# A scan phase whose matmul order is written out by a planner of two streams, with whole groups of small matmuls, instead of left to the scheduler

## The chip, the cores and the metric

One core of one Trainium2 chip runs the whole program in one launch. The metric is device time in microseconds (us), the median over runs. TensorE is called PE here, its weight loads PEld, VectorE DVE, ScalarE ACT, GpSimd POOL, and SyncE, which issues the DMAs, SP.

## The reference, cut to what matters

The program computes two layers of a hybrid block over 512 tokens, 256 latent and 256 context, of width 1024. Each layer is a gated feed-forward half step, a token mixer of three branches (grouped attention, a two-way RWKV-7 scan, neighbourhood attention) and a second feed-forward half step. The change is in the RWKV branch:

```python
def rwkv_scan(state0, xs, emit):
    def step(state, inp):
        r_t, w_t, k_t, v_t, a_t, b_t = inp
        sa = einsum('zbhvk,zbhk->zbhv', state, a_t)
        state = state * w_t + sa * b_t + v_t * k_t
        out = einsum('zbhvk,zbhk->zbhv', state, r_t)
        return state, out
    return lax.scan(step, state0, xs)

y_ctx = scan(zeros, context tokens);  y = scan(state after the context, latent tokens)
readout: (group_norm(o forward + o backward) + bonus) * g
```

It has 8 heads of 64 channels and two directions z, forward and backward. The gates of the merge are `sigmoid(u @ w_in[gate columns])`, one 1024-wide set for each branch.

## The kernel before, in words

Channels lie on the 128 partitions, tokens along the free axis. Each large product is made from values split in two: `wload` (L262, L263) or `split` (L278, L279) turns a weight tile into a high part (ACT copy, `whi` or `phi`) and a low part (DVE subtraction, `wlo` or `plo`), and `gemm` (L272 to L274) issues three matmuls for each 128 rows of weights, on 512 columns (256 in layer 1 where only the latent tokens are needed).

The RWKV branch (`rwkv`) is the **scan phase** of a layer. It begins with four projections (`ps_first`), and then works on four **pairs** of heads, `ct` = 0 to 3, each in these stages:

- `rwkv_prep`: three projections of the pair (`proj`: k, v, r), a token shift of each, the key's norm (`rstd`: `ps_ss`, a POOL power, `ps_bc`), values per chunk (`ps_v` into `X`), the bonus; then `rwkv_dir` for each direction z: the decay and rate products (`ps_w` L949, `ps_a` L953), activations and a running sum, then `bk`, the two keys in one tile. `gram` (`ps_g`, L1041, evacuated to `G` at L1045) makes the 64x64 blocks of 8 chunks; then DVE multiplies `bk` in place by the chunk's decay (L1003) and PE transposes it (`ps_kb`, L1011).
- `inverse`: triangular inverses of the 64x64 blocks. DVE cuts the 16x16 diagonal blocks out (L1076), a DMA through DRAM lays those of both directions into one tile `N`, 15 steps of two tiny DVE instructions (L1096, L1098) invert them all, a DMA through DRAM brings them back (`cc`). Then for z = 0 and after it for z = 1: DVE masks `G` to `lt` (L1120), and five groups of small matmuls with an evacuation between each two: `ps_x`, `ps_it`, `ps_iw` (64x64), `ps_x2`, `ps_w2` (32x32), all five in the one bank `ia`.
- `rwkv_chain`, `chain_steps`: eight serial steps over the chunks. A step is four small matmuls `ps_z` (L1182), an ACT copy `zs`, four `ps_u` (L1203), copies into `X` (ACT L1205, DVE L1206), four `ps_h` (L1210), a DVE add into the next `X` (L1218); outputs `ps_oo` (L1191, L1224) beside them. `hq` (L1197) is the state times the chunk's decay, four DVE instructions a step.
- `rwkv_out`: the group norm and the gate (`ps_gg`, L1241); the result `yf` stays in SBUF until the attention phase.

The small products are in plain fp32, and a row of the trace counts two records for one such matmul.

**Fillers.** 42 projections that the rest of the mixer needs (queries, keys, values of the attention branches, gates) are cut into 8 **quanta** each, 336 in a layer (`spare_quanta`): a quantum is three matmuls `ps_gate` (L773 to L775), and after the eighth the tile goes to DRAM (`pd`). `fill(n)` emits n of them; `FILL` says how many after each pair, `LEFT` (8 and 2 tiles) how many are kept for the attention phase.

**What sets the order.** The kernel is written in Tile, whose scheduler arranges each engine's instructions from the order of emission, the dependences and a priority; `prio(-30)` is around the chain. So PE's order, one matmul at a time, is the scheduler's:

```python
            if ct < 3:
                for _ in self.rwkv_prep(ct + 1, nxt):
                    pass
                self.inverse(nxt["z"])
            with self.prio(-30):
                for _ in chain:
                    pass
            self.rwkv_out(ct, st, po, y)
            self.fill(min(8 * FILL[l][1 + ct], len(self.fq) - 8 * LEFT[l]))
```

Of the kernel before, what the change touches and what calls it, by code (L numbers as in the profile page):

```python
# [7 lines left out]
F32 = mybir.dt.float32  # L8
# [35 lines left out]
FILL = [[5, 7, 3, 4, 24], [8, 5, 4, 4, 24]]  # L44
# [7 lines left out]
    0, 4, 5, 6, 10, 14, 18, 19, 20, 21, 25, 29, 33)  # L52


class Program:
# [261 lines left out]
    def rstd(self, sqs, n, cols, scale, eps, tag="aux"):  # L317
# [5 lines left out]
        for k, sq in enumerate(sqs):  # L323
            for b in range(n):
# [5 lines left out]
                                in1=self.mhalf[:, 0:n * w].rearrange("p (n w) -> p n w", n=n), op=ALU.pow)  # L330
        bc = self.bank(tag, [P, n * P], "ps_bc")
# [193 lines left out]
    def proj(self, tile_i, full):  # L525

        nc = self.nc
        pt = self.bank("mm", [P, NT], "ps_p")
        for h in range(2):
            raw = self.rp.tile([P, NT], F32, tag="praw", name="praw", bufs=2)  # L530
# [3 lines left out]
            w = [[t[:, P * k:P * k + P] for k in range(4)] for t in (wh, wl)]  # L534
            self.gemm(pt[:, full], w, [t[:, full] for t in self.uh[4 * h:4 * h + 4]],
                      [t[:, full] for t in self.ul[4 * h:4 * h + 4]], h == 0, h == 1)
        return pt
# [265 lines left out]
    def fill(self, n):  # L803

        for _ in range(min(n, len(self.fq))):
            self.fq.pop(0)()


    def shift(self, i, full, pt=None):

        nc, l = self.nc, self.l
        if pt is None:
            pt = self.proj(T_R + i, full)
# [13 lines left out]
    def t(self):  # L827
        return self.rp.tile([P, NT], F32, tag="t", name="t", bufs=4)

    def rwkv(self):  # L830
# [25 lines left out]
        for h in HALVES:  # L856
            for w, pt in zip(ws, pts):
# [5 lines left out]
        self.gdt = self.shift(T_GD - T_R, tok)  # L863
        nc.scalar.activation(out=self.gdt[:, tok], in_=self.gdt[:, tok], func=AF.Tanh, scale=0.5)
        nc.vector.tensor_scalar(out=self.gdt[:, tok], in0=self.gdt[:, tok], scalar1=0.5, scalar2=0.5,
                                op0=ALU.mult, op1=ALU.add)
        self.fq = self.spare_quanta()
        self.fill_to = self.rp, "gm"
        st = {}
        y = []  # L870
        for _ in self.rwkv_prep(0, st):
            pass
        self.inverse(st["z"])
        self.fill(8 * FILL[l][0])
        for ct in range(4):
            nxt = {}
            po, chain = self.rwkv_chain(ct, st)

            if ct < 3:
                for _ in self.rwkv_prep(ct + 1, nxt):  # L880
                    pass
                self.inverse(nxt["z"])
            with self.prio(-30):
                for _ in chain:
                    pass
            self.rwkv_out(ct, st, po, y)
            self.fill(min(8 * FILL[l][1 + ct], len(self.fq) - 8 * LEFT[l]))
            st = nxt
        self.fill(len(self.fq) - 8 * LEFT[l])
        return y  # L890

    def rwkv_prep(self, ct, st):
        nc, l, tok, need = self.nc, self.l, self.tok, self.need
        pr = self.rwp[:, l]
        lora = self.rp.tile([P, 2, P], F32, tag="lora", name="lora")
        nc.sync.dma_start(out=lora, in_=self.A["lora"][l, ct][:, 0:2, :])
        g2 = self.rp.tile([P, P], F32, tag="g2", name="g2")
        nc.sync.dma_start(out=g2, in_=self.A["lora"][l, ct][:, 2, :])
        pk, pv = self.kv0 if ct == 0 else (None, None)
        k = self.shift(T_RK - T_R + ct, FULL, pk)  # L900
        yield
        v = self.shift(T_RV - T_R + ct, FULL, pv)
        yield
        r = self.shift(ct, tok)
        yield
        sq = self.t()
        nc.scalar.activation(out=sq, in_=k, func=AF.Square, scale=pr[:, 4, ct:ct + 1])
        bc = self.rstd([sq], 4, self.hsel, 1.0, 1e-12)
        kk = self.rp.tile([P, NT], F32, tag="kk", name="kk", bufs=1)
        nc.vector.scalar_tensor_tensor(out=kk, in0=k, scalar=pr[:, 4, ct:ct + 1], in1=bc, op0=ALU.mult, op1=ALU.mult)  # L910
        st.update(g2=g2)
        yield
# [9 lines left out]
        for p in range(2):  # L922
            o = slice(HD * (1 - p), HD * (1 - p) + HD)
            nc.scalar.activation(out=X[o, 0:4, 0, p, :], in_=pv[o, 4:8, :], func=AF.Copy)
            nc.scalar.activation(out=X[o, 4:8, 0, p, :], in_=pv[o, 0:4, :], func=AF.Copy)
            nc.vector.tensor_copy(X[o, :, 1, p, :], pv[o, ::-1, :])
        st["X"] = X
# [7 lines left out]
        st["z"] = []  # L935
        for z in range(2):
            yield
            st["z"].append((yield from self.rwkv_dir(ct, z, r, k, kk, lora)))

    def rwkv_dir(self, ct, z, r, k, kk, lora):  # L940
        nc, l, tok, need = self.nc, self.l, self.tok, self.need
        pr = self.rwp[:, l]
        rows = slice(64 * z, 64 * z + 64)
# [4 lines left out]
        pw = self.bank("aux", [P, NT], "ps_w")  # L948
        nc.tensor.matmul(pw, lora[rows, 0, :], self.wdt[rows, :], start=True, stop=True)  # L949
        sw = self.t()  # L950
        nc.scalar.activation(out=sw, in_=pw, func=AF.Tanh, scale=0.5, bias=self.wah[:, l, z, ct:ct + 1])
        pa = self.bank("aux", [P, NT], "ps_a")
        nc.tensor.matmul(pa, lora[rows, 1, :], self.adt[rows, :], start=True, stop=True)  # L953
        ta = self.t()
        nc.scalar.activation(out=ta, in_=pa, func=AF.Tanh, scale=0.5, bias=self.wah[:, l, 2 + z, ct:ct + 1])
        nc.gpsimd.tensor_scalar(out=sw, in0=sw, scalar1=1.0, scalar2=None, op0=ALU.add)
        S = self.t()
# [13 lines left out]
        yield  # L971
        inv = self.t()
# [3 lines left out]
        pc = self.rp.tile([P, NCH], F32, tag="pc", name="pc", bufs=4)  # L976
        nc.vector.tensor_copy(pc, ch(Q)[:, :, last])
# [14 lines left out]
        bk = self.rp.tile([P, NCH, 2, C], F32, tag="bk", name="bk", bufs=1)  # L992
# [4 lines left out]
        yield  # L997
        G = self.gram(z, bk, ar)
        yield

        pcb = pc.unsqueeze(2).to_broadcast([P, NCH, C])
        for x in range(2):
            nc.vector.tensor_tensor(out=bk[:, :, x, :], in0=bk[:, :, x, :], in1=pcb, op=ALU.mult)  # L1003
        kb = []
        flat = bk.rearrange("p j x t -> p (j x t)")
        for p in range(2):
            h = slice(HD * p, HD * p + HD)
            pt = self.bank("aux", [P, NCH, C], "ps_kb")
            t = self.lp.tile([P, NCH, C], F32, tag="kb", name="kb", bufs=5)
# [13 lines left out]
        return dict(ar=ar, kb=kb, G=G, pc=pc)  # L1023

    def gram(self, z, bk, ar):


        nc = self.nc
        nr = NCH if self.need else NCH // 2
# [18 lines left out]
        return G  # L1048
# [7 lines left out]
    def it(self):  # L1056
        return self.rp.tile([P, NT], F32, tag="it", name="it", bufs=3)

    def inverse(self, dirs):


        nc, tc = self.nc, self.tc
        halves = [slice(0, HD), slice(HD, P)]

        def ch(a):
            return a.rearrange("p (j t) -> p j t", t=C)

        dn = tc.dram_tile([NCH, 2, P, 16], F32, name="dn")
        dr = tc.dram_tile([2, NCH, 2, P, 16], F32, name="dr")
        for z in range(2):  # L1070
            G = dirs[z]["G"]
            e = self.it()
            for p in range(2):
                h = halves[p]
                for jh in range(2):
                    nc.vector.tensor_tensor(  # L1076
                        out=ch(e)[h, 4 * jh:4 * jh + 4].rearrange("p j (b t) -> p j b t", b=4),
                        in0=G[p][jh][h, :, 0:C].rearrange("p j (b t) -> p j b t", b=4),
                        in1=self.mblk[h].unsqueeze(1).unsqueeze(3).to_broadcast([HD, 4, 4, 16]), op=ALU.mult)
            if z == 1:  # L1080
                e1 = self.it()
                nc.vector.transpose(e1, e)
                e = e1
            ec = self.rp.tile([P, NCH, 16], F32, tag="ec", name="ec", bufs=2)
            nc.vector.tensor_reduce(out=ec, in_=e.rearrange("p (j b t) -> p j t b", j=NCH, b=4), axis=AX.X, op=ALU.add)
            nc.sync.dma_start(out=dn[:, z].rearrange("j g t -> g j t"), in_=ec)
        N = self.rp.tile([P, 16, 16], F32, tag="N", name="N", bufs=1)
        nc.sync.dma_start(out=N, in_=dn.rearrange("j z (g s) t -> (j z g) (s t)", s=16))
# [13 lines left out]
        for z in range(2):  # L1102
            d = dirs[z]
            G = d["G"]
            full = []
            for tag, i, bufs in (("W", z, 4), ("T", 1 - z, 1)):
                c = self.rp.tile([P, NCH, 16], F32, tag="ec", name="cc", bufs=2)
                nc.sync.dma_start(out=c, in_=dr[i, :, z].rearrange("j g t -> g j t"))
                t = self.rp.tile([P, NCH, C], F32, tag=tag, name=tag, bufs=bufs) if tag == "W" else ch(self.it())
                nc.vector.tensor_tensor(  # L1110
                    out=t.rearrange("p j (b t) -> p j b t", b=4),
                    in0=c.unsqueeze(2).to_broadcast([P, NCH, 4, 16]),
                    in1=self.mblk.unsqueeze(1).unsqueeze(3).to_broadcast([P, NCH, 4, 16]), op=ALU.mult)
                full.append(t)
            W, T = full
            lt = ch(self.it())
            for p in range(2):
                h = halves[p]
                for jh in range(2):
# [20 lines left out]
            def rows(p, blk):  # L1140
                return slice(HD * p + blk.start, HD * p + blk.stop)
# [307 lines left out]
```

## Time and profile before

| | |
|---|---|
| median of 3 runs | 2935.11 us (2932.16 to 2943.57) |
| the profiled execution's own time | 2933.89 us |
| its span in the profile | 2932.1 us |
| mean granted clock of TensorE, full speed as 1 | 0.971 |
| PE, DVE, ACT, POOL busy, share of the span | 95%, 60%, 36%, 9% |
| layer 0, first `ps_first` to last `ps_gg` | 426.48 to 963.92 us |
| layer 1, first `ps_first` to last `ps_gg` | 2071.21 to 2538.92 us |

A row of the timeline merges neighbouring instructions of one group (xN); its start is measured, a matmul's end is modelled, so what a matmul costs PE is read from the distance between starts. A share of busy time is a mean over stages with different limits.

### The profile page before, as it was taken

How to read it: one execution, taken by the hardware profiler on the slowest of the kernel's cores; microseconds unless marked ns; L12 is line 12 of the kernel's file. 1: busy time of each engine (PE TensorE's matmuls, PEld its weight loads, DVE VectorE, ACT ScalarE, POOL GpSimd, SP SyncE). 2: the span in 40 equal slices, each digit the busy share in tenths (PEclk: the TensorE clock that was granted, in tenths of full speed). 3: DMA queues.
4: the chain of work that ended last, by engine and by line, in shares of the span. 5: the costliest groups of instructions: out<-in, count | busy, mean ns of one | idle time of the engine just before them, and what ended most of it. 6: DMA issues, size and time to landing. Idle time of an engine off the chain costs nothing. (4 is left out here: it accounts for less than half of the span.)

```text
span 2932.1 us, 48565 instructions
## 1 busy us (share of the span) xinstructions
PE 2795.4 (95%) x19654; PEld 2229.4 (76%) x19654; DVE 1766.0 (60%) x3023; ACT 1068.6 (36%) x1928; POOL 277.6 (9%) x274
## 2 busy tenths in 40 slices
PE   7999999999999899999999999999899999898998
PEld 5788887656666666697888888888876678777998
DVE  4667346756674256757673477633578777485654
ACT  3223235323232246433222333222543433374543
POOL 0000011100000111230000110001210110022000
PEclk8999999999999999999999999999999999799998
DMA  7555343221112433336553365433432224344654
GB/s 277 201 187 170 107 134 105 76 69 44 41 58 73 133 108 110 105 119 215 171 181 106 119 201 183 147 102 107 141 114 69 70 60 119 104 130 138 218 177 144
DMA packets 205311, 376.59 MB, mean 128 GB/s; under 512 B 79776, under 2 KB 109088, under 8 KB 205088
## 3 DMA queue, kind: packets, MB, share of 16 engines
q1 hardware_dynamic: 205088, 373.51, 41.1%
q8 instruction: 154, 2.52, 0.4%
q14 instruction: 69, 0.57, 0.1%
HBM read 340.93 MB, written 31.46 MB: 127 GB/s over the span
## 5 line engine op out<-in xcount | busy, mean ns | idle before, releaser
L262 ACT ACTIVATE whi<-raw 128x1024 fp32r<-128x1024 f32 (+1 forms) x399 | 415.1, 1041 | 1102.5 <-PE ps_o L273 297.5
L263 DVE TENSOR_TENSOR wlo<-raw,whi 128x1024 fp32r<-128x1024 f32 (+1 forms) x399 | 500.4, 1255 | 425.1 <-ACT whi L262 415.8
L195 DVE SCALAR_TENSOR_TENSOR acc<-araw,cs,acc 128x1024 f32<-128x1024 f32 x210 | 260.6, 1279 | 14.3 <-DMA araw<-in_w_ada 14.0
L272 PE MATMUL ps_o<-hh,whi 128*128 128x512 f32 (+1 forms) x770 | 268.8, 349 | 0.0
L274 PE MATMUL ps_o<-hh,wlo 128*128 128x512 f32 (+1 forms) x770 | 268.0, 348 | 0.0
L273 PE MATMUL ps_o<-hl,whi 128*128 128x512 f32 (+1 forms) x770 | 266.6, 346 | 0.0
L272 PE MATMUL ps_fg<-uh,whi 128*128 128x512 f32 (+1 forms) x704 | 255.4, 363 | 7.3 <-ACT whi L262 3.7
L773 PE MATMUL ps_gate<-uh,whi 128*128 128x512 f32 (+1 forms) x672 | 255.6, 380 | 3.1 <-ACT whi L262 3.1
L274 PE MATMUL ps_fu<-uh,wlo 128*128 128x512 f32 (+1 forms) x704 | 251.9, 358 | 5.1 <-DVE wlo L263 5.1
L774 PE MATMUL ps_gate<-ul,whi 128*128 128x512 f32 (+1 forms) x672 | 256.0, 381 | 0.0
L274 PE MATMUL ps_fg<-uh,wlo 128*128 128x512 f32 (+1 forms) x704 | 253.4, 360 | 1.7 <-DVE wlo L263 1.7
L775 PE MATMUL ps_gate<-uh,wlo 128*128 128x512 f32 (+1 forms) x672 | 254.4, 379 | 0.7 <-DVE wlo L263 0.6
L273 PE MATMUL ps_fg<-ul,whi 128*128 128x512 f32 (+1 forms) x704 | 252.7, 359 | 0.1
L272 PE MATMUL ps_fu<-uh,whi 128*128 128x512 f32 (+1 forms) x704 | 251.2, 357 | 0.9 <-ACT whi L262 0.9
L273 PE MATMUL ps_fu<-ul,whi 128*128 128x512 f32 (+1 forms) x704 | 250.9, 356 | 0.0
L272 PEld LDWEIGHTS ps_fg<-uh,whi 128*128 128x128 f32 x704 | 134.8, 191 | 38.3 <-ACT whi L262 12.0
L272 PEld LDWEIGHTS ps_o<-hh,whi 128*128 128x128 f32 x770 | 144.7, 188 | 20.4 <-ACT whi L262 1.7
L273 PEld LDWEIGHTS ps_o<-hl,whi 128*128 128x128 f32 x770 | 144.5, 188 | 20.1
L274 PEld LDWEIGHTS ps_o<-hh,wlo 128*128 128x128 f32 x770 | 144.7, 188 | 18.2
L274 PEld LDWEIGHTS ps_fu<-uh,wlo 128*128 128x128 f32 x704 | 133.7, 190 | 26.6 <-DVE wlo L263 8.0
L773 PEld LDWEIGHTS ps_gate<-uh,whi 128*128 128x128 f32 x672 | 130.2, 194 | 28.3 <-issue 5.7
L274 PEld LDWEIGHTS ps_fg<-uh,wlo 128*128 128x128 f32 x704 | 134.7, 191 | 22.2 <-DVE wlo L263 3.0
(298 smaller groups left out, 5270.2 us busy)
## 6 DMA issues: line engine op xcount, KB each, us to landing
raw<-in_ffn_wi SPq DMA_DIRECT2D x176, 512.0 KB, 3.6
araw<-in_w_ada SPq DMA_DIRECT2D x144, 512.0 KB, 3.8
raw<-in_w_in SPq DMA_DIRECT2D x92, 512.0 KB, 3.7
raw<-in_ffn_wo SPq DMA_DIRECT2D x70, 448.0 KB, 3.3
raw<-in_ffn_wo SPq DMA_DIRECT2D x35, 512.0 KB, 3.5
pd<-fg SPq DMA_DIRECT2D x52, 256.0 KB, 2.0
raw<-in_w_branch SPq DMA_DIRECT2D x24, 512.0 KB, 3.8
praw<-in_w_in SPq DMA_DIRECT2D x44, 256.0 KB, 2.8
```

The source lines that it names most:

```text
L195: nc.vector.scalar_tensor_tensor(out=a, in0=raw, scalar=c, in1=a, op0=ALU.mult, op1=ALU.add)
L262: nc.scalar.activation(out=hi[:, :m], in_=r, func=AF.Copy)
L263: self.lo = nc.vector.tensor_tensor(out=lo[:, :m], in0=r, in1=hi[:, :m].bitcast(F32), op=ALU.subtract)
L272: nc.tensor.matmul(pt, wh, xh[k], start=first and k == 0, stop=False)
L273: nc.tensor.matmul(pt, wh, xl[k], start=False, stop=False)
L274: nc.tensor.matmul(pt, wl, xh[k], start=False, stop=last and k == n - 1)
L773: nc.tensor.matmul(pt, wh, xh, start=k == 0, stop=False)
L774: nc.tensor.matmul(pt, wh, xl, start=False, stop=False)
L775: nc.tensor.matmul(pt, wl, xh, start=False, stop=k == KD - 1)
```

## The change

The scan phase's PE order becomes the program's own. `tc.manual_schedule` takes PE from the scheduler between `ps_first` and the end of the phase; the other engines stay with it. The stages are generators: each `yield cost, after` ends a **whole group** of PE work, with an estimate of its length and of the time until the next group's inputs are there. `Streams.step` keeps a clock of its own and takes the first stream that is ready within 0.3, the chain ahead of the preparation; with none ready it emits one quantum (counted as 1.0, in layer 1 0.75). What the order rests on are these estimates, not semaphores. Beside that:

- two streams: `chains()` runs the four chains, `preps()` the directions, gram, keys and inverses; for a pair, `blocks(ct)` (the 16x16 step and the inverses) runs beside `rest(ct)` (keys of z = 1, and the three projections, norm and values of pair ct + 1). `preps` waits for the half of the chain of ct - 1 before the gram of z = 1.
- both directions' `ps_w` and `ps_a` come in pairs of banks; the two inverses go group by group side by side, z = 0 in bank `ia`, z = 1 in `aux`.
- the mask moves from `G` (DVE, four instructions per direction) to the evacuation of `ps_x`, which moves from ACT to DVE with it.
- `bk` times the decay moves from DVE to POOL and stands behind the last gram matmul that reads `bk`.
- `hq` is two DVE instructions for a step instead of four.
- `FILL` is gone; quanta that no gap took are emitted behind the phase. `LEFT` is as before.
- `yf` goes to DRAM (`yd`) and comes back in the attention phase, 4 DMAs each way and layer; `proj` takes its raw weights in the shared `raw` tiles; buffers: `t` 5 (4), `it` 4 (3), `bk` 2 (1), `kb` 6 (5).

```diff
+class Streams:
+    NEAR = 0.3
...
+    def par(self, *gens):
+        ready = {g: self.t for g in gens}
+        while ready:
+            g = min(ready, key=ready.get)
...
+                cost, after = next(g)
...
+            end = self.t + cost
+            ready[g] = end + after
+            yield cost, max(0.0, min(ready.values()) - end)
+
+    def step(self, streams):
...
+        g = next((g for g in live if self.ready.get(g, 0.0) <= self.t + self.NEAR), None)
+        if g is None and self.fill(1):
+            self.t += self.cost
+            return True
+        if g is None:
+            g = min(live, key=lambda g: self.ready[g])
+        self.t = max(self.t, self.ready.get(g, 0.0))
...
+            cost, after = next(g)
...
+        self.t += cost
+        self.ready[g] = self.t + after
...
+        mix = Streams(lambda n: len(self.fq) > left and self.fill(n), 1.0 if need else 0.75)
...
+        def blocks(ct):
+            st = sts[ct]
+            yield from self.blocks16(st)
+            yield from mix.par(*[self.inverse(st, z, ("ia", "aux")[z]) for z in range(2)])
+            done["prep"] = ct
+
+        def rest(ct):
+            while done["chain"] < ct - 1:
+                yield 0.0, 0.5
+            yield from self.keys(sts[ct]["z"][1])
+            if ct < 3:
+                yield from heads(ct + 1)
...
+            for ct in range(4):
+                st = sts[ct]
+                yield from self.rwkv_dirs(ct, st)
+                yield from self.gram(st, 0)
+                yield from self.keys(st["z"][0])
+                while done["half"] < ct - 1:
+                    yield 0.0, 0.5
+                yield from self.gram(st, 1)
+                yield from mix.par(blocks(ct), rest(ct))
...
+        streams = [chains(), preps()]
+        with self.tc.manual_schedule(engines={mybir.EngineType.PE}):
+            while mix.step(streams):
+                pass
+        self.fill(len(self.fq) - left)
...
-        pcb = pc.unsqueeze(2).to_broadcast([P, NCH, C])
-        for x in range(2):
-            nc.vector.tensor_tensor(out=bk[:, :, x, :], in0=bk[:, :, x, :], in1=pcb, op=ALU.mult)
...
+            if jh == 0:
+                pcb = d["pj"].unsqueeze(2).to_broadcast([P, NCH, C])
+                for x in range(2):
+                    nc.gpsimd.tensor_tensor(out=bk[:, :, x, :], in0=bk[:, :, x, :], in1=pcb, op=ALU.mult)
+            yield 1.2, 1.4
...
+        yield 0.0, 23.0
...
-                    nc.vector.tensor_tensor(out=lt[h, 4 * jh:4 * jh + 4], in0=G[p][jh][h, :, 0:C],
-                                            in1=self.mlev[h, z, :].unsqueeze(1).to_broadcast([HD, 4, C]), op=ALU.mult)
...
-            px = mm("ps_x", lt, T)
-            nc.scalar.activation(out=X, in_=px, func=AF.Copy)
+        px = mm("ps_x", lambda p, h, j: G[p][j // 4][h, j % 4, 0:C], T)
+        nc.vector.tensor_tensor(out=X, in0=px, in1=self.mlev[:, z, :].unsqueeze(1).to_broadcast([P, NCH, C]),
+                                op=ALU.mult)
+        yield 1.15, 1.1
...
-                    for z, p in units:
-                        nc.vector.tensor_scalar(out=hq[halves[p], z, :], in0=X[halves[p], s, z, p, :],
...
+                    for h in halves:
+                        nc.vector.tensor_tensor(
+                            out=hq[h], in0=X[h, s, :, halves.index(h), :],
+                            in1=st["pc"][h, s, :].unsqueeze(2).to_broadcast([HD, 2, C]), op=ALU.mult)
+            yield (s, 0.45, 0.8) if first else (s, 0.9, 0.4)
...
+            yield s, 0.45, 0.9
...
+            yield (s, 0.9, 1.0) if out else (s, 0.45, 1.4)
...
+        nc.sync.dma_start(out=self.yd[ct][:, tok], in_=os_[:, tok])
...
+                    yf = self.mp.tile([P, NT], F32, tag="qk", name="yf", bufs=4)
+                    nc.sync.dma_start(out=yf[:, tok], in_=self.yd[ct][:, tok])
```

What the change moves on PE is seen at two places. **Chain.** PE in layer 0, the chain of pair 0, before: the seventh step, from its `ps_oo` (L1191) on; `ps_gate` are quanta.

```order
L1191 MATMUL ps_oo<-ar,X 64x64 x3
L774 MATMUL ps_gate<-ul,whi 128x512
L775 MATMUL ps_gate<-uh,wlo 128x512
L773 MATMUL ps_gate<-uh,whi 128x512
L1203 MATMUL ps_u<-zs,W 64x64
L774 MATMUL ps_gate<-ul,whi 128x512
L1203 MATMUL ps_u<-zs,W 64x64
L775 MATMUL ps_gate<-uh,wlo 128x512
L1203 MATMUL ps_u<-zs,W 64x64
L773 MATMUL ps_gate<-uh,whi 128x512
L1203 MATMUL ps_u<-zs,W 64x64
```

The same chain now, one step from its `ps_z` (L1325) to its `ps_h` (L1353):

```order
L1325 MATMUL ps_z<-X,G 64x64 x4
L1333 MATMUL ps_oo<-ar,X 64x64 x4
L834 MATMUL ps_gate<-uh,whi 128x512
L835 MATMUL ps_gate<-ul,whi 128x512
L836 MATMUL ps_gate<-uh,wlo 128x512
L1346 MATMUL ps_u<-zs,W 64x64 x4
L834 MATMUL ps_gate<-uh,whi 128x512
L835 MATMUL ps_gate<-ul,whi 128x512
L836 MATMUL ps_gate<-uh,wlo 128x512
L1353 MATMUL ps_h<-X,kb 64x64 x4
```

Before, four matmuls of `ps_u` stand one by one among quantum matmuls; now each of the chain's groups stands whole, with one quantum of three matmuls between two groups.

**Inverse.** PE in layer 0, the inverse of pair 0, z = 0, before (L1127 are its 64x64 groups, 16 matmuls each; `ps_bo`, `ps_w` belong to the preparation of pair 1):

```order
L1127 MATMUL ps_x<-it 64x64
L773 MATMUL ps_gate<-uh,whi 128x512
L774 MATMUL ps_gate<-ul,whi 128x512
L1127 MATMUL ps_x<-it 64x64 x15
L775 MATMUL ps_gate<-uh,wlo 128x512
L773 MATMUL ps_gate<-uh,whi 128x512
L774 MATMUL ps_gate<-ul,whi 128x512
L775 MATMUL ps_gate<-uh,wlo 128x512
L1127 MATMUL ps_it<-it,W 64x64 x16
```

The inverses of pair 0 now (L1267 the 64x64 groups of both directions, L1291 the 32x32 ones; `ps_p` is a projection, `ps_ss`, `ps_bc`, `ps_v` belong to the norm and values of pair 1):

```order
L321 MATMUL ps_p<-uh,plo 128x512
L1267 MATMUL ps_x<-it,G 64x64 x32
L1267 MATMUL ps_it<-it,W 64x64 x16
L381 MATMUL ps_ss<-c_hsel,t 128x2 x4
L1267 MATMUL ps_it<-it,W 64x64 x16
L1267 MATMUL ps_iw<-W,it 64x64 x32
L395 MATMUL ps_bc<-c_ident,rs 64x128 x8
L1291 MATMUL ps_x_4432<-it,G 32x32 x16
L1032 MATMUL ps_v<-c_center,sh 64x64 x16
L1291 MATMUL ps_x_4476<-it,G 32x32 x16
```

Before, one direction's groups come with quanta between them and a single matmul ahead of the other fifteen; now the groups of z = 0 and z = 1 stand next to each other, and other small groups of pair 1 lie between them.

## Rows read from the trace of the kernel before

**Rows 1.** The page, part 1: busy time, share of the span, instructions.

```profile
PE 2795.4 (95%) x19654; PEld 2229.4 (76%) x19654; DVE 1766.0 (60%) x3023; ACT 1068.6 (36%) x1928; POOL 277.6 (9%) x274
```

**Rows 2.** Windows: stretch, us, PE, PEld, DVE, ACT, POOL, PEclk, DMA share, GB/s.

```profile
427.00:1010.00 583.00, 558.28 (x4894) 391.52 (x4892) 342.89 (x758) 198.55 (x388) 54.92 (x46) 0.98 0.26 76
2070.00:2540.00 470.00, 436.24 (x4715) 344.73 (x4713) 333.69 (x756) 194.95 (x394) 52.77 (x50) 0.94 0.32 92
...
2520.00:2540.00 20.00, 15.44 (x148) 12.12 (x144) 7.13 (x24) 3.52 (x12) 1.12 (x1) 0.50 0.01 3
```

**Rows 3.** Timeline, PE, layer 0: start, us, engine, line, names, form, xN.

```profile
603.98 0.40 PE L774 MATMUL ps_gate<-ul,whi 128*128 128x512 f32 x1
604.21 0.40 PE L775 MATMUL ps_gate<-uh,wlo 128*128 128x512 f32 x1
...
625.23 0.33 PE L1203 MATMUL ps_u<-zs,W 64*64 64x64 f32 x2
625.49 0.49 PE L775 MATMUL ps_gate<-uh,wlo 128*128 128x512 f32 x1
625.91 0.33 PE L1203 MATMUL ps_u<-zs,W 64*64 64x64 f32 x2
...
601.87 0.45 PE L1203 MATMUL ps_u<-zs,W 64*64 64x64 f32 x8
602.25 0.51 PE L775 MATMUL ps_gate<-uh,wlo 128*128 128x512 f32 x1
...
572.17 1.15 PE L1127 MATMUL ps_it<-it,W 64*64 64x64 f32 x32
573.25 0.50 PE L773 MATMUL ps_gate<-uh,whi 128*128 128x512 f32 x1
```

**Rows 4.** Timeline, PE, layer 1: quanta on 256 columns.

```profile
2513.92 0.28 PE L774 MATMUL ps_gate<-ul,whi 128*128 128x256 f32 x1
2514.04 0.28 PE L775 MATMUL ps_gate<-uh,wlo 128*128 128x256 f32 x1
```

**Rows 5.** Timeline, ACT and PE, layer 0, pair 0: `ps_w` evacuated, first gram.

```profile
484.86 0.69 ACT L951 ACTIVATE t<-ps_w,wah 128x512 f32<-128x512 f32 x1 [2.56 <-PE ps_w L949]
...
496.31 0.89 PE L1041 MATMUL ps_g<-ar,bk 64*64 64x128 f32 x24 [1.33 <-DVE bk L996]
```

**Rows 6.** Timeline, PE and DVE, pair 0: second gram to inverse.

```profile
523.82 0.50 PE L774 MATMUL ps_gate<-ul,whi 128*128 128x512 f32 x1
...
555.92 0.27 PE L1127 MATMUL ps_x<-it 64*64 64x64 f32 x1
...
544.64 0.18 DVE L1098 TENSOR_TENSOR R<-R,tm 128x15 f32<-128x15 f32 x1
547.51 0.37 DVE L1099 COPY N<-R 128x256 f32<-128x256 f32 x1
```

**Rows 7.** Timeline, PE and ACT, pair 0: hops of a chain step.

```profile
593.58 0.45 PE L1210 MATMUL ps_h<-X,kb 128*64 128x64 f32 x8 [0.76 <-DVE X L1206]
595.54 0.45 PE L1182 MATMUL ps_z<-X,G 128*64 128x64 f32 x8
596.04 0.28 ACT L1186 ACTIVATE zs<-ps_z 128x128 f32<-128x128 f32 x1
```

**Rows 8.** One line, L991 on POOL, and the timeline of POOL and DVE there.

```profile
L991 POOL TENSOR_TENSOR t<-t,sh x16: 1274/1782/2208, 492.0 to 2423.8; 128x512 f32<-128x512 f32 x16
...
492.00 2.20 POOL L991 TENSOR_TENSOR t<-t,sh 128x512 f32<-128x512 f32 x1 [4.86 <-DVE t L989]
...
491.83 1.22 DVE L263 TENSOR_TENSOR wlo<-raw,whi 128x1024 fp32r<-128x1024 f32 x1
```

**Rows 9.** Lines of DVE, by form: xcount, busy us, mean ns, idle before.

```profile
L1197 DVE TENSOR_SCALAR hq<-X,pc 64x64 f32<-64x64 f32 x192 | 49.4, 257 | 4.0
L1120 DVE TENSOR_TENSOR it<-G,c_mlev 64x256 f32<-64x256 f32 x64 | 24.1, 416 | 0.4
L1003 DVE TENSOR_TENSOR bk<-bk,pc 128x512 f32<-128x512 f32 x32 | 21.8, 687 | 11.7 <-PE ps_g L1041 11.6
```

More of the change, by code (lines that the diff above doesn't have):

```diff
@@ L315, in stats_add, with rstd, rstd_steps @@
             nc.gpsimd.tensor_tensor(out=self.zs[:, h], in0=self.zs[:, h], in1=self.z[m][:, h], op=ALU.add)
-    def rstd(self, sqs, n, cols, scale, eps, tag="aux"):
+    def rstd(self, *args, **kw):
+        steps = self.rstd_steps(*args, **kw)
+        while True:
+            try:
+                next(steps)
+            except StopIteration as e:
+                return e.value
+    def rstd_steps(self, sqs, n, cols, scale, eps, tag="aux", after=3.2):
         nc = self.nc
@@ L873, in rwkv @@
[L873 to L877, printed above, removed]
-            if ct < 3:
[L880 to L888, printed above, removed]
@@ L889, in rwkv, with heads @@
-        self.fill(len(self.fq) - 8 * LEFT[l])
-        return y
-    def rwkv_prep(self, ct, st):
+        left = 8 * LEFT[l]
+        self.yd = self.tc.dram_tile([4, P, NT], F32, name=f"yd{l}")
+        sts = [{} for _ in range(4)]
+        done = {"prep": -1, "half": -1, "chain": -1}
+        mix = Streams(lambda n: len(self.fq) > left and self.fill(n), 1.0 if need else 0.75)
+        def heads(ct):
+            yield from self.rwkv_proj(ct, sts[ct])
+            yield from self.rwkv_tokens(ct, sts[ct])
@@ new lines, in chains @@
+        def chains():
+            for ct in range(4):
+                while done["prep"] < ct:
+                    yield 0.0, 0.5
+                with self.prio(200):
+                    po = self.bank("po", [P, NCH, C], "ps_oo")
+                steps = self.chain_steps(sts[ct], po)
+                while True:
+                    with self.prio(200):
+                        try:
+                            s, *said = next(steps)
+                        except StopIteration:
+                            break
+                    if s == NCH // 2:
+                        done["half"] = ct
+                    yield said
+                yield from self.rwkv_out(ct, sts[ct], po)
+                done["chain"] = ct
@@ L934, in rwkv_prep, with rwkv_dirs, rwkv_dir @@
         st["bonus"] = bonus
[L935 to L940, printed above, removed]
+        yield 1.1, 0.2
+    def rwkv_dirs(self, ct, st):
+        nc, l = self.nc, self.l
+        lora = st["lora"]
+        lows = [[], []]
+        first = [self.t() for _ in range(4)]
+        second = [self.t() for _ in range(2)]
+        for i, (x, w) in enumerate(((self.wdt, 0), (self.adt, 2))):
+            pts = [self.bank("aux", [P, NT], "ps_w") for _ in range(2)]
+            for z in range(2):
+                rows = slice(64 * z, 64 * z + 64)
+                nc.tensor.matmul(pts[z], lora[rows, i, :], x[rows, :], start=True, stop=True)
+            for z in range(2):
+                t = first[i] if z == 0 else second[i]
+                nc.scalar.activation(out=t, in_=pts[z], func=AF.Tanh, scale=0.5,
+                                     bias=self.wah[:, l, w + z, ct:ct + 1])
+                lows[z].append(t)
+            yield 2.1, 0.0 if i == 0 else 12.0
+        st["pc"] = self.rp.tile([P, NCH, 2], F32, tag="pc", name="pc", bufs=2)
+        st["z"] = [self.rwkv_dir(ct, z, st, *lows[z], *(first[2:] if z == 0 else [self.t() for _ in range(2)]))
+                   for z in range(2)]
+    def rwkv_dir(self, ct, z, st, sw, ta, S, inv):
         nc, l, tok, need = self.nc, self.l, self.tok, self.need
         pr = self.rwp[:, l]
-        rows = slice(64 * z, 64 * z + 64)
+        r, k, kk = st["r"], st["k"], st["kk"]
         def ch(a):
             return a.rearrange("p (j t) -> p j t", t=C)
[L948 to L955, printed above, removed]
         nc.gpsimd.tensor_scalar(out=sw, in0=sw, scalar1=1.0, scalar2=None, op0=ALU.add)
-        S = self.t()
         nc.vector.tensor_tensor_scan(S, self.scan0, sw, 0.0, ALU.mult, ALU.add)
@@ L1143, in inverse @@
-            px = self.bank("ia", [P, NCH, 32], "ps_x2")
-            for j in range(NCH):
-                for p in range(2):
-                    nc.tensor.matmul(px[rows(p, b), j, :], G[p][j // 4][rows(p, a), j % 4, b], T[rows(p, a), j, a],
-                                     start=True, stop=True)
-            X = self.it()[:, 0:NCH * 32].rearrange("p (j t) -> p j t", t=32)
-            for p, eng in ((0, nc.scalar), (1, nc.vector)):
-                self.copy(eng, X[rows(p, b)], px[rows(p, b)])
```

308 lines of the change are left out of this document (175 added, 133 removed).

## The prediction

> **What bounds the kernel now.** I read the page's busy shares first: PE is busy 95% of the span, the next engine, DVE, 60% [rows 1]. So the program is a list of matmuls, and it gets shorter in two ways only: PE waits less, or the same matmuls take PE less time. The windows over the two scan stretches show how much the first way has to give: PE is busy 558.28 of 583 us in layer 0 and 436.24 of 470 us in layer 1 [rows 2], so it waits 24.7 + 33.8 = 58.5 us in both. The second way is in the timeline. Two quantum matmuls that follow each other start 0.23 us apart (603.98, 604.21). Where one small matmul of a chain stands between quanta, a whole period of small one and quantum one takes 625.91 - 625.23 = 0.68 us [rows 3]. A small matmul among its own kind takes 1.08 / 16 = 0.07 us (572.17 to 573.25). So a lone small matmul makes PE lose 0.68 - 0.23 - 0.07 = 0.38 us that neither product needs. Four together: they take 0.38 us (601.87 to 602.25) where four bare ones are 0.27, and the quantum matmul between two such visits takes 0.42 us (625.49 to 625.91) instead of 0.23; together 0.30 us lost [rows 3]. The loss is paid per visit, hardly per matmul. PE's busy time hides it, since the slow switch counts as busy. The reader should also see the last 20 us of layer 1's stretch: PE busy 15.44 us at a granted clock of 0.50, the lower of its two levels, where the last chain has little beside it [rows 2].
>
> **Whole groups.** I counted, in the orders of both kernels, the visits of small matmuls between ordinary ones, from the first projection of the phase to its last output: 305 in layer 0 before and 108 now, 187 and 113 in layer 1, with the same small matmuls. 271 visits go. Visits of a single matmul fall from 157 to 2 and from 52 to 2, so 205 of the 271 are single ones. Cost removed: 205 x 0.38 + 66 x 0.30 = 98 us. All at the cheaper or all at the dearer price give 81 and 103 us.
>
> **Quanta move.** The order shows 95 more quanta behind the last output of layer 0 and 161 more in layer 1 (there were 43 and 0). On 512 columns a quantum is 3 x 0.23 = 0.69 us, on 256 columns 3 x 0.12 = 0.36 us [rows 3, 4]. That is 95 x 0.69 + 161 x 0.36 = 123.6 us of work taken out from beside the chains. By itself this costs nothing, as it is done either way; what it costs is cover. In exchange layer 1's last chain is followed at once by dense work. I count that as 8 us: 15.44 us of work at half the clock would be 7.7 at the full one.
>
> **New waits.** In a fixed order PE stands where the next group's inputs are late, and everything behind it stands too, both streams alike. I go through a pair:
> - Decay products to gram. Before, the first `ps_w` was evacuated at 484.86 and the gram began at 496.31, 11.45 us later [rows 5]. The order now puts about 8.6 us of PE work there (rows 3's prices for what it lists). Wait: 3 us.
> - Gram to keys. Two POOL multiplies stand in this path now. The nearest row is a POOL product of the same 128x512, 1.27 to 2.21 us [rows 8], so 2.5 to 4.4 us against two quanta, 1.4 us, and a switch. Wait: 2 us. On DVE they took 0.69 us each [rows 9].
> - Second gram to inverse. It took 555.92 - 523.82 = 32.1 us [rows 6]. From this go the copy's delay (its last input was there at 544.82, it began at 547.51: 2.7 us in which DVE stood behind another instruction), the four masks (4 x 0.42 = 1.7) and the two multiplies (1.4) [rows 9]: about 26.3 us. The order has 20 to 22.5 us of work there. Wait: 5 us.
> - Chain. From `ps_h` to the next `ps_z` it is 595.54 - 593.58 = 1.96 us, and from `ps_z` to the end of its copy 596.04 + 0.28 - 595.54 = 0.78 us [rows 7]. A quantum and the groups themselves fill about 1.3 us, so the long hop waits 0.65 us and the two short ones nothing in layer 0. In layer 1 a quantum is 0.33 us shorter: about 0.95 and twice 0.15. The mean is 0.3 us, 24 hops: 7 us.
> - Inverse. Five groups of two directions, each covered by the other's: 2 us.
>
> Together 19 us a pair, 152 us for 8 pairs. It isn't additive, since a wait in one stream lets the other's inputs mature: between half, 76, and all of it I take two thirds, 101 us. Against the 58.5 us of now that is +43 us.
>
> **The rest at nothing.** DVE loses the masks (24.1 us), about half of `hq` (49.4) and the multiplies (21.8) over the run [rows 9], and gains some 11 us of evacuation; DVE is busy 59% and 71% of the stretches [rows 2], so this is cover, not path, except for what I have taken off the second gram's path. If DVE's queue were late in the chain's copies, it would be a gain of a few us in the hops. The 8 stores and 8 loads of `yd` (256 KB at most) move while DMA is busy 0.26 to 0.32 of the time [rows 2]; the loads are wanted after 138 and 161 quanta, far behind the stores. If that cover were gone, one load would show once a layer. Deeper buffers can only remove waits.
>
> **Sum.** -98 - 8 + 43 = -63 us on the profiled 2933.9 us: 2871. The median of the runs lies 1.2 us above the profiled execution, so 2872 us.
>
> **Rivals.**
> - *Everything covered.* The planner's estimates hold and PE waits no more than now. For it: it leaves quanta to spare, so it never ran out of cover. Against it: the four gaps above are longer than the work listed in them. 2935 - 98 - 8 = 2829 us.
> - *POOL holds DVE up.* The one row that shows both at work: a POOL product issued 0.17 us into a two-input DVE subtraction took 2.20 us where the shortest of its kind took 1.27 [rows 8]. If it goes the other way too, each of the 32 multiplies that move to POOL stops DVE's evacuations for its own length, 32 x 1.27 = 41 us, on a path with no slack. 2872 + 41 = 2913 us. Against it: DVE has idle time to catch up in, and the chain's first copy is on ACT. The Trainium skill, "SBUF — State Buffer", section "Who interferes with whom", speaks for it: a DVE instruction with two inputs in SBUF contends with a GpSimd one that reads SBUF, and the one that issues second is blocked in full. The trace agrees in the direction it shows, 2.20 against 1.27 us.
> - *Every hop late.* All 192 hops wait 0.65 us as the long one: 77 us more, two thirds of it 51. 2923 us, within the 0.5% (14.7 us) that a measurement of this kernel can tell from no change. For it: copies of the chain stand in DVE's and ACT's queues behind 0.6 to 1.3 us instructions of the preparation.
> - *A pair's latency sets the end; slower.* If a pair's own path (directions, gram, 16x16 blocks, inverse, then the half of the chain that the next gram waits for) is the period, then PE's saving becomes idle time, and the 123.6 us of quanta that moved out are done behind it in addition. The point at which it decides: each of the 8 pairs must be shorter by 123.6 / 8 = 15.5 us to break even; the forecast makes it (63 + 123.6) / 8 = 23. With 10 us it is (15.5 - 10) x 8 = +44: 2979 us. For it: PE still has its list of quanta when the phase ends, so the phase ended by latency, at least in the planner's clock. Against it: the gaps above sum to well under the 100 us and more that a pair takes now.
>
> **Chances.** Forecast 0.54, all covered 0.17, POOL 0.11, late hops 0.10, latency 0.08. Faster by over 0.5%: the first three, 0.82; within: 0.10; slower: 0.08. The forecast's own bounds, half or all of the waits, are 2847 and 2923. The range reaches from a little under the covered case, 2820, to 2922, and leaves out the last two, 0.18.
>
> **What would show it.** Right: rows of quanta 0.23 us apart between whole groups; PE's waits in the stretches near 100 us, led by `ps_x` behind DVE or the DMA, `ps_g` behind `bk`, `ps_z` behind `X`, `ps_kb` behind POOL; dense `ps_gate` behind the last `ps_gg` and the clock near 1 there. Wrong: waits over 200 us (latency), POOL's multiplies near 2.2 us with DVE idle beside them (POOL), or visits that still cost 0.6 us each although they are whole, so that the 98 us are not there.

## The result, and the profile after

The changed kernel takes 3034.06 us (median of 4 runs, 3022.93 to 3040.09) against 2933.64 us beside it: a ratio of 1.0335, 95% interval 1.0292 to 1.0378. It is 3.4% slower; 2872 us had been forecast.

The page, part 1, of the changed kernel (beside [rows 1]), and the windows over its two scan stretches, first `ps_first` to last `ps_gg` (beside [rows 2], same columns):

```profile
PE 2769.0 (91%) x19654; PEld 2249.3 (74%) x19654; DVE 1729.8 (57%) x2871; ACT 1061.8 (35%) x1912; POOL 308.1 (10%) x306
```

```profile
427.00:928.00 501.00, 414.99 (x4422) 308.60 (x4420) 298.14 (x657) 162.21 (x337) 69.54 (x61) 0.85 0.20 58
2124.00:2580.00 456.00, 379.38 (x4236) 296.81 (x4237) 286.88 (x655) 160.74 (x341) 64.49 (x66) 0.82 0.23 65
```

PE's busy time fell by 26 us, and the span grew by 101. From first projection to last output the stretches went from 537.4 to 500.7 us and from 467.7 to 453.8: 51 us shorter. But 124 us of quanta had moved out of them. That is 73 us lost, and 28 us more elsewhere. The waits by group (lines of PE in layer 0's stretch: xcount, busy us, mean ns, idle before and what ended it):

```profile
L1267 PE MATMUL ps_x<-it,G 64*64 64x64 f32 x256 | 15.2, 306 | 24.3 <-DVE it L1256 24.3
L1171 PE MATMUL ps_g<-ar,bk 64*64 64x128 f32 x512 | 27.1, 338 | 15.6 <-DVE bk L1124 10.6 <-DVE G L1175 2.9 <-DVE kb L1148 2.0
L1138 PE MATMUL ps_kb<-c_ident,bk 64*128 64x64 f32 x120 | 11.1, 256 | 12.9 <-DVE G L1175 7.3 <-POOL bk L1181 4.2 <-ACT kb L1140 1.4
```

They wait where the prediction said, for longer: 162.6 us in both stretches, where 54.0 were before. What follows a wait can be slow as well. PE in layer 0 in pair 0's inverses, by the timeline, and a window right behind them:

```profile
557.55 1.97 PE L1267 MATMUL ps_x<-it,G 64*64 64x64 f32 x32 [3.27 <-DVE it L1256]
...
570.04 1.48 PE L1045 MATMUL ps_bo<-bonus,c_hdiag 128*128 128x512 f32 x2 [1.83 <-DVE it L1190]
```

```profile
575.00:580.00 5.00, 5.00 (x24) 2.13 (x22) 2.31 (x2) 2.74 (x5) 2.95 (x2) 0.50 0.02 3
```

Waits of 3.27 and 1.83 us with only small matmuls around them, and the five busy us behind stand at 0.50, the lower level.

Where a visit can be read, it became as cheap as forecast. A chain step between quanta, PE, layer 0: from `ps_u` to `ps_h` it is 586.88 - 585.61 = 1.27 us for four matmuls (0.27) and a quantum (0.69), so a whole group costs 0.31 us beside its work, 0.30 in the prediction:

```profile
585.61 0.45 PE L1346 MATMUL ps_u<-zs,W 64*64 64x64 f32 x8
585.99 0.50 PE L834 MATMUL ps_gate<-uh,whi 128*128 128x512 f32 x1
...
586.88 0.45 PE L1353 MATMUL ps_h<-X,kb 128*64 128x64 f32 x8
```

At the border to the attention phase PE waits 10.58 us in layer 0 and 8.97 us in layer 1 for the first load of `yf`; in layer 0 of the kernel before PE waits 1.41 us ahead of `ps_b`. The last quantum behind the phase, the load and the wait (timeline, layer 0):

```profile
1021.84 0.39 PE L836 MATMUL ps_gate<-uh,wlo 128*128 128x512 f32 x1
...
1027.49 1.86 SPq L1417 DMA_DIRECT2D yf<-yd  x4
1032.13 1.15 ACT L325 ACTIVATE yh<-yf 128x512 fp32r<-128x512 f32 x2 [8.55 <-DMA yf<-yd]
...
1032.81 0.79 PE L319 MATMUL ps_b<-yh,whi 128*128 128x512 f32 x1 [10.58 <-ACT yh L325]
```

### The profile page after: what moved, and what is told of

It is laid out like the page before. It is cut to its first block, busy times and chain, and to the rows that moved or that the text cites. A ratio compares the mean times of both kernels' runs of the same rounds, so it can differ in the third digit from the quotient of the medians.

```text
span 3033.5 us, 48469 instructions
## 1 busy us (share of the span) xinstructions
PE 2769.0 (91%) x19654; PEld 2249.3 (74%) x19654; DVE 1729.8 (57%) x2871; ACT 1061.8 (35%) x1912; POOL 308.1 (10%) x306
## 4 chain that ended last, share of the span: by engine, by line
PE 42%; DVE 5%; DMA 3%; ACT 2%; issue 2%; POOL 1%; SPq 0%; ACTq 0%; POOLq 0%; DVEq 0%
PE ps_o L319 3%; PE ps_o L321 3%; PE ps_o L320 3%; PE ps_fu L321 3%; PE ps_fg L319 3%; PE ps_fu L320 3%; PE ps_fu L319 3%; PE ps_fg L321 3%; PE ps_fg L320 3%; PE ps_gate L834 2%; PE ps_gate L835 1%; PE ps_gate L836 1%; DMA araw<-in_w_ada 1%; DVE acc L242 1%; DVE wlo L310 1%
## 5 line engine op out<-in xcount | busy, mean ns | idle before, releaser
L834 PE MATMUL ps_gate<-uh,whi 128*128 128x512 f32 (+1 forms) x672 | 268.2, 399 | 3.8 <-ACT whi L309 3.8
L836 PE MATMUL ps_gate<-uh,wlo 128*128 128x512 f32 (+1 forms) x672 | 245.7, 366 | 1.1 <-DVE wlo L310 1.1
L835 PE MATMUL ps_gate<-ul,whi 128*128 128x512 f32 (+1 forms) x672 | 246.5, 367 | 0.0
```

The costliest lines, as they stand in the source:

```text
L834: nc.tensor.matmul(pt, wh, xh, start=k == 0, stop=False)
L835: nc.tensor.matmul(pt, wh, xl, start=False, stop=False)
L836: nc.tensor.matmul(pt, wl, xh, start=False, stop=k == KD - 1)
```

## The experiments

Three theories: A, a wait costs its length and then work at the low clock; B, its length alone; C, **latency**: a pair's own path, from its decay products to its inverses, sets the **period**, the time from one pair to the next. Ratios are to the kernel before, run beside each.

**The quanta taken out** (e11).

```diff
-        mix = Streams(lambda n: len(self.fq) > left and self.fill(n), 1.0 if need else 0.75)
+        mix = Streams(lambda n: 0, 1.0 if need else 0.75)
```

> The changed kernel with no quanta in the planned order: the 116 and 140 that the planner put in are done behind the phases, where they take 116 x 0.69 + 140 x 0.36 = 130 us. Theory throughput (the stretch is as long as PE's work in it plus separate waits): the stretches get shorter by what moved out, and the time stays near 3034. Theory latency (a pair's own path, decay products to the end of the inverses, is the period): the stretches stay near 500 and 454 us, with over 100 us more of waits, and the time rises by 90 to 130 us, to 3125 to 3165.

3177.97 us, 1.0813 (1.079 to 1.0836), 13 us above the range that C had given. The stretches are 497.7 and 449.5 us with 256 quanta fewer, as good as unchanged; PE's busy time in them fell by 120 us, and its waits rose by 113 us to 275. The windows over the stretches:

```profile
427.00:924.00 497.00, 359.58 (x4067) 279.45 (x4067) 281.48 (x642) 139.86 (x304) 66.23 (x61) 0.69 0.14 36
2192.00:2642.00 450.00, 312.20 (x3801) 247.95 (x3802) 268.67 (x636) 137.03 (x306) 64.56 (x63) 0.69 0.15 39
```

The first `ps_z` of each of the four pairs' chains shows the same, layer 1, PE's timeline of the kernel before, the changed one and this one:

```profile
2196.24 0.33 PE L1182 MATMUL ps_z<-X,G 64*64 64x64 f32 x2
...
2282.95 0.33 PE L1182 MATMUL ps_z<-X,G 64*64 64x64 f32 x2
...
2370.50 0.45 PE L1182 MATMUL ps_z<-X,G 64*64 64x64 f32 x8
...
2461.86 0.45 PE L1182 MATMUL ps_z<-X,G 64*64 64x64 f32 x8
```

```profile
2259.68 0.70 PE L1325 MATMUL ps_z<-X,G 64*64 64x64 f32 x8
...
2343.99 0.45 PE L1325 MATMUL ps_z<-X,G 64*64 64x64 f32 x8
...
2454.52 0.69 PE L1325 MATMUL ps_z<-X,G 64*64 64x64 f32 x8
...
2534.02 0.69 PE L1325 MATMUL ps_z<-X,G 64*64 64x64 f32 x8
```

```profile
2330.49 0.69 PE L1325 MATMUL ps_z<-X,G 64*64 64x64 f32 x8
...
2414.85 0.45 PE L1325 MATMUL ps_z<-X,G 64*64 64x64 f32 x8
...
2525.99 0.69 PE L1325 MATMUL ps_z<-X,G 64*64 64x64 f32 x8
...
2604.23 0.49 PE L1325 MATMUL ps_z<-X,G 64*64 64x64 f32 x8
```

Pair to pair: 86.7, 87.6 and 91.4 us before; 84.3, 110.5 and 79.5 changed; 84.4, 111.1 and 78.2 with the quanta out. In layer 0 it is 135.1, 115.7 and 88.5 before, 92.2, 126.3 and 85.5 changed, and 93.8, 124.5 and 84.5 with the quanta out. So the quanta are not what sets the changed order's period: latency. One thing is not separated: the clock fell to 0.69 in both stretches, so the groups on the path ran slower too, and without that the path might have been a little shorter. In layer 1 the kernel before had no longer a period (88.5 us in the mean, 91.4 changed), with 320 quanta inside.

**More quanta in the gaps** (e5, e8: other numbers in the planner).

```diff
-            self.t += self.cost
+            self.t += self.more if self.ran else self.cost
...
-            yield 2.1, 0.0 if i == 0 else 12.0
+            yield 2.1, 0.0 if i == 0 else 16.0
...
-            yield 1.2, 1.4
+            yield 1.2, 1.4 if jh else 5.0
...
-        yield 0.0, 23.0
+        yield 0.0, 31.0
```

The diff is e5's: `more` is 0.69, in layer 1 0.36. In e8 the 16 is 21, the 31 is 42, and the gap behind `ps_u` grows from 0.9 to 1.4.

> The changed kernel with other numbers in its planner: a quantum behind a quantum counts 0.69 (layer 1: 0.36) instead of 1.0 (0.75), the gaps behind the decay products, the gram and the 16x16 step count 16, 5 and 31 instead of 12, 1.4 and 23. 25 and 37 more quanta stand inside the two stretches. The profile of the changed kernel has 162 us of PE waits in the stretches (54 before) and a granted clock of 0.85 and 0.82 there (0.98 and 0.94 before). Theory A (a wait costs its length and then work at the low clock): 25 x 0.69 + 37 x 0.36 = 31 us of waits go, the clock rises to about 0.90, and the time falls by about twice the waits, 60 us, to about 2975. Theory B (waits cost their length alone): the time falls by 31 us, to about 3003, whatever the clock does. Theory C (a pair's latency is the period): the waits go elsewhere in the pair, the time falls by 31 us at most, and PE waits in the stretches stay near 162 us less 31.

> e5 with still larger gaps in the planner: 21 instead of 16 behind the decay products, 42 instead of 31 behind the 16x16 step, 1.4 instead of 0.9 behind ps_u. 42 and 49 quanta more than in e5 stand inside the stretches. Theory A: another 30 us or more of waits go, and with the clock the time falls by 50 us, to about 2930. Theory latency: the added quanta bring their own weight splits to DVE and ACT, on which the 16x16 step and the chain's copies stand, so the waits fall by less than the quanta's own 46 us and the time falls by under 25 us.

2982.52 us, 1.0151 (1.0115 to 1.0186), and 2962.57 us, 1.0078 (1.0057 to 1.01). e5's waits fell by 30 us and the time by 52, between A's 60 and B's 31, and more than the 31 that C had allowed. Layer 1's stretch was 453.8, 455.5 and 454.7 us with 158, 195 and 244 quanta inside (changed kernel, e5, e8): what goes in there is free, by C. Layer 0 is less clear: 500.7, 483.7 and 508.3 us with 134, 159 and 201. e8's gain of 20 is under the 25 that C gave it; A's 50 did not come.

**Clock alone** (e6): the useless matmul `nc.tensor.matmul(pt, self.uh[0][:, 0:P], self.uh[0], start=True, stop=True)`, 8 times ahead of each pair's first gram, 8 ahead of its first keys and 16 ahead of its first `ps_x`.

> The changed kernel, with useless matmuls (128x512, overwritten by the group behind them) ahead of three groups of each pair that wait: 8 ahead of the first gram, 8 ahead of the first keys, 16 ahead of the first ps_x, 256 in all, some 7.4 us a pair at 0.23 us each. The inputs of the groups come no earlier. Theory A: the clock in the stretches rises above 0.90, and the time falls by 30 to 60 us although PE does more. Theory B or C: the same time, or up to 20 us more where a useless matmul stands in the way.

3035.67 us, 1.0333 (1.0299 to 1.0367): no change in the sum. In layer 0 the clock rose from 0.85 to 0.93, and the stretch fell from 500.7 to 481.1 us though PE did 29 us of useless work; in layer 1 the clock rose from 0.82 to 0.86 and the stretch from 453.8 to 472.4, with the waits at `ps_kb` up from 10.0 to 23.1 us, 21.7 of it ahead of the useless matmuls, which needed a bank that DVE was still emptying of the gram. So in layer 0 the low clock is a part of the loss; its share in the sum stays open. The windows of e6:

```profile
426.00:907.00 481.00, 421.64 (x4549) 312.73 (x4549) 296.13 (x657) 162.04 (x338) 71.90 (x62) 0.93 0.22 61
2100.00:2573.00 473.00, 403.69 (x4352) 313.81 (x4352) 291.60 (x654) 159.47 (x340) 64.29 (x64) 0.86 0.22 62
```

**PE's order left to the scheduler** (e7): `with nullcontext():` in place of `manual_schedule`.

> The changed kernel with PE's order left to the scheduler again: the same program, streams and emission, without manual_schedule. The order has 86 and 53 visits of small matmuls instead of 107 and 112, and 134 and 158 quanta behind the phases. Theory order (the fixed order puts too little work ahead of the late groups): the scheduler puts its own amount there, PE's waits in the stretches fall well below 162 us and the time lies between 2880 and 2960. Theory latency (a pair's own path is the period whatever PE does): waits of 130 us or more stay, and the time stays within 20 us of 3034.

3013.55 us, 1.0263 (1.0221 to 1.0305). Both were half wrong: waits fell to 93.9 us, yet the stretches were still 478.4 and 451.4 us, at a clock of 0.86 and 0.79. Fewer waits did not make it fast; the fixed order alone isn't the cause either.

**Keys on DVE again** (e3): `nc.vector` for `nc.gpsimd` in `gram`.

> The changed kernel with bk times the decay on DVE again instead of POOL, in the same place. Theory POOL (it holds DVE's instructions up): DVE's instructions beside it get shorter and the time falls by 40 us or more. Theory A: only the waits of the key transposes on POOL go, 6.9 us in the stretches, and with the clock 10 to 15 us at most; the mean length of DVE's instructions stays as it is.

3049.92 us, 1.0375 (1.0335 to 1.0416): neither the 40 us of the POOL theory nor A's 10 to 15. POOL isn't it: its 32 multiplies took 1.04 us (median), and on DVE the waits of `ps_kb` doubled, from 22.9 to 45.7 us.

**The border** (e4: `yd` put into the kernel before; e9: in the changed kernel 24 quanta moved behind it).

```diff
-        self.fill(len(self.fq) - left)
+        self.fill(len(self.fq) - left - 24)
...
                 self.psum(ctx, f"m1{l}", mm=2, s=2, t=1, o=1)
+                self.fill_to = self.mp, "mm"
+                self.fill(24)
```

> The kernel before, with the scan's result stored to DRAM and loaded again in the attention phase, as in the changed kernel, and nothing else. In the changed kernel PE waits 10.6 us in layer 0 and about 9 us in layer 1 for that load at the border of the phases. Theory border (the loads stand behind the release of the scan's buffers, so nothing covers them): 20 us more, and up to 30 with the clock. Theory hidden (the prediction's): no difference.

> The changed kernel, with 24 of the quanta that stand behind each scan phase moved to the first place of the attention phase, ahead of the loads of yd. Nothing else. Theory border: the 10.6 and 9 us for which PE waits there are covered, and the time falls by 20 to 25 us. Theory hidden: no difference.

2962.59 us, 1.009 (1.0059 to 1.0121), and 3009.3 us, 1.0239 (1.0212 to 1.0267): some 25 us each way. In e4 PE now waits at the border, 9.88 us in layer 0 (below) and 7.14 in layer 1; in e9 no wait of 1 us is left ahead of `ps_b`. Shown from both sides.

```profile
1011.15 0.80 PE L272 MATMUL ps_b<-yh,whi 128*128 128x512 f32 x1 [9.88 <-ACT yh L278]
```

**Together** (e10: e8 and e9).

> e8 and e9 together. If the two causes are independent, the gains of both add up: by theory A about 2905, faster than the kernel before; by theory latency about 2940.

2931.91 us, 0.998 (0.9964 to 0.9996): level with the kernel before, and near C's 2940, not A's 2905. Quanta back in the gaps and the border covered give back the whole loss.

**The path shortened** (e12: the projections at the head of `rest`; e15: the decay products of the next pair at its end; e16: both, the diff below; e13, e14, e17: the same three on e10).

```diff
+            if ct < 3:
+                yield from self.rwkv_proj(ct + 1, sts[ct + 1])
             while done["chain"] < ct - 1:
                 yield 0.0, 0.5
             yield from self.keys(sts[ct]["z"][1])
             if ct < 3:
-                yield from heads(ct + 1)
+                yield from self.rwkv_tokens(ct + 1, sts[ct + 1])
+                yield from self.rwkv_dirs(ct + 1, sts[ct + 1])
...
-                yield from self.rwkv_dirs(ct, st)
+                if ct == 0:
+                    yield from self.rwkv_dirs(ct, st)
```

> The changed kernel with the next pair's three projections at the head of rest(ct), ahead of the wait for the chain of ct - 1, instead of behind it. In the changed kernel's trace the decay products of pair 2 begin 38 us (layer 0) and 27 us (layer 1) behind the end of pair 1's inverses, while the other pairs follow at once. Theory latency: that gap closes, the stretches get shorter by 40 to 65 us together, and the time falls by the same, less for the quanta that lose their place, to about 2985. Theory throughput: the order of PE's work changes, not its sum: within 15 us of 3034.

> The changed kernel with the next pair's decay products and what follows them on DVE, ACT and POOL emitted at the end of rest(ct), beside the inverses, instead of behind them. In the changed kernel's trace a pair's decay products begin as the inverses of the pair before end, and the gram follows them by about 20 us, in all pairs but the first. Theory latency (that path is the period): 10 to 15 us go from each of 6 pairs, 60 to 90 us, and the time is 2945 to 2975. Theory waits and clock alone (PE's order leaves it waiting, whoever is late): the same work and as many late groups, within 20 us of 3034.

> The changed kernel with both moves: the next pair's projections at the head of rest(ct) (as in e12) and its decay products at its end (as in e15). In e15 the decay products came only 3 to 6 us ahead of the end of the inverses and pair 2 was as late as before, so the path was not shortened. With the projections early they can come some 15 us ahead. Theory latency: the stretches get shorter by 50 to 80 us together; 19 and 15 quanta fewer lie inside, which costs 13 + 5 = 18 us behind; the time is 2970 to 3000. Theory waits alone: within 20 us of 3034.

3036.37, 3042.83 and 3045.79 us, ratios 1.0339, 1.0362, 1.0365: no gain, and each expectation of theory C missed. e12 closed 38 us to 15 in layer 0, whose stretch fell by 11 us, but layer 1's grew by 5, and 29 quanta left the stretches, 14 us. e16's stretches are 480.6 and 471.3 us: 20 less in layer 0, 17 more in layer 1. The traces give two reasons. First, e16 hardly did what it was meant to do. Pair 1's decay products start 8.2 and 7.6 us ahead of the end of pair 0's inverses (layers 0 and 1), but pair 2's start 12.1 and 7.1 us behind the end of pair 1's, and pair 3's 7.7 behind and 3.9 ahead. Second, where they are early, in pair 1, the first `ps_z` of pairs 0 and 1 still lie 2348.53 - 2262.97 = 85.6 us apart. PE in layer 1 of e16: the first and the fifth `ps_z` of pair 0, the gram of z = 1 of pair 1, its inverses, its first `ps_z`, and the decay products of pair 2:

```profile
2262.97 0.64 PE L1329 MATMUL ps_z<-X,G 64*64 64x64 f32 x8
...
2292.13 0.70 PE L1329 MATMUL ps_z<-X,G 128*64 128x64 f32 x8
...
2293.04 0.37 PE L1175 MATMUL ps_g<-ar,bk 64*64 64x64 f32 x2
...
2326.76 1.98 PE L1271 MATMUL ps_x<-it,G 64*64 64x64 f32 x32 [4.56 <-DVE it L1260]
...
2344.58 1.74 PE L1304 MATMUL ps_w<-W,it 32*32 32x32 f32 x64
...
2348.53 0.69 PE L1329 MATMUL ps_z<-X,G 64*64 64x64 f32 x8
...
2353.39 1.73 PE L1065 MATMUL ps_w<-sh,lora 64*128 64x512 f32 x4
```

So there is a second loop of the same length. Half of the chain, 30.1 us, comes first, since the planner holds the gram of z = 1 back until then (its `G` buffers come free with that half). From that gram over the 16x16 step to the first `ps_x` it is 33.7 us, and over the inverses to the next chain 21.8. I had taken one of two paths for the only one.

> e10 (larger gaps in the planner, border covered) with the projections early as in e12. In e10's trace pair 2 already follows pair 1 at once, so by theory latency there is little left to close: within 15 us of e10's 2932, with the sign open.

> e10 (larger gaps, border covered, 2932 us) with the same early decay products. Theory latency: the path is shorter in 6 pairs, and more quanta lie inside the stretches than in e15, so PE becomes the bound in layer 0 first: 30 to 60 us less, 2875 to 2905. Theory waits and clock alone: within 15 us of 2932.

> e14 (2914 us) with the projections at the head of rest(ct). 28 quanta in layer 0 and 29 in layer 1 leave the stretches, 30 us. Theory latency: the path gets a little shorter, the stretches by 20 to 40 us, so the time is within 15 us of e14's. Theory waits alone: 15 to 30 us more than e14.

2935.72, 2914.33 and 2907.56 us: 1.0002 (0.9983 to 1.002), 0.9927 (0.9901 to 0.9953) and 0.9894 (0.9862 to 0.9927). e13 and e17 came out where C had them; e14 gained 18 us, between the two theories. **e17 is faster than both kernels**, by 1.1% and 4.3% (0.9894 / 1.0335). Its windows, the second from 3 us behind the start of its stretch:

```profile
427.00:892.00 465.00, 412.03 (x4553) 310.22 (x4553) 303.55 (x665) 171.92 (x350) 67.41 (x66) 0.94 0.25 71
2040.00:2480.00 440.00, 383.70 (x4401) 308.90 (x4402) 291.81 (x654) 168.46 (x349) 63.71 (x59) 0.87 0.27 77
```

463.7 and 442.2 us by first and last group, with 177 and 221 quanta inside; in layer 1 the pairs lie 88.4, 87.7 and 73.5 us apart, where e10 had 96.9, 102.4 and 84.9. Why the early decay products pay here and not in the changed kernel was not tried apart, but the traces differ in this: in e17 they start 13.5 to 26.6 us ahead of the end of the inverses in all six pairs. In layer 1, pair 2's decay products and the last group of pair 1's inverses:

```profile
2256.00 1.12 PE L1069 MATMUL ps_w<-sh,lora 64*128 64x512 f32 x2 [0.52 <-DVE bonus L1054]
...
2274.26 1.52 PE L1308 MATMUL ps_w<-W,it 32*32 32x32 f32 x64 [0.70 <-DVE it L1198]
```

## Why the prediction was wrong

- *Visits, 98 us*: right in the price where one was read, 0.31 for 0.30 us. The step that failed is what it was taken to buy: the sum set PE's saving against PE's waits as if PE were the bound of each pair.
- *Quanta move, "costs nothing, as it is done either way"*: the false term. It is done behind stretches that hardly shrink. The latency rival had the right sum: to break even each of 8 pairs must shorten by 15.5 us; the stretches shortened by 36.7 + 13.9 = 50.6 us, 6.3 a pair, so 123.6 - 50.6 = 73 us are lost. It got 0.08, since "the gaps above sum to well under the 100 us and more that a pair takes now". That sum left out the half of the chain that the next gram waits for, though the rival itself named it, and layer 1 took 88.5 us a pair, not 100: with the path as it was, there was little to take out. The sign that it had set for latency, waits over 200 us, did not come either: they were 162.6 us.
- *New waits, 101 us*: 162.6 us. They are no independent cause: taking PE's work away made more of them (e11).
- *`yd` at nothing*: about 25 us (e4, e9). The text named the loads' cover as the quanta behind the phase; but the loads are issued at 1027.49, 5 us behind the end of that work; by the kernel's pools their buffers lie where the scan's were, and the quanta still used those.
- *Clock*: a gain of 8 us was counted. It fell to 0.85 and 0.82 over both stretches. By difference, -124 (quanta) - 98 (visits) + 108 (waits) would shorten the stretches by 114 us; they shortened by 51. The 63 us between are PE work that took longer than counted; that this is mostly the low clock is argued, and e6 shows it in layer 0 alone.
- *POOL*: 41 us that did not come (e3). The rule in the Trainium skill, "SBUF — State Buffer", section "Who interferes with whom", may hold, but no run here shows a price for it.
- *Two sums*: the 58.5 us of waits before come from a window that ends 46 us behind layer 0's phase; in the stretches they were 54.0. Late hops, by the prediction's own mean, would cost 192 x 0.65 - 56 = 69 us, not 77. Neither decides anything.

## What to carry to other kernels

Before pricing an engine's list, read the period from the trace: the distance between the same group of neighbouring units (86.7, 87.6 and 91.4 us here), and the path that ties them, buffers that come free included. If the period is already that path, work taken from beside it is work added behind it. Ask of a load where its buffer lies: it can't be hidden behind work that still holds the memory.

## What the runs showed of the hardware that was not expected

The granted clock fell to 0.85 and 0.82 in stretches where PE was busy 83% of the time, and with the quanta out to 0.69, with PE busy 72% and 69%. Fewer waits alone did not raise it: in e7, with 93.9 us of waits and about as many quanta inside (138 and 162), it was 0.86 and 0.79; the changed kernel had 162.6 us of waits, 134 and 158 quanta, 0.85 and 0.82. Nor do the quanta inside order it: in layer 0 it was 0.94 in e17 with 177 and 0.89 in e8 with 201. What decides it stays open. A multiply of 128x512 took 1.04 us on POOL (median of 32, its second operand a broadcast) where the nearest row before had 1.27 to 2.21.
